# Two of four column blocks of an output projection as seven products of halves, with sums of weights made by DMA during the recurrence

## The chip, the cores and the metric

The kernel runs on one core of one Trainium2 chip. The metric is the device time of one execution in microseconds. The profile is of one execution, taken by the hardware profiler.

## What is computed

One layer of a hybrid trunk over 512 positions of width 2048, in fp32:

```python
h = rms_norm(x, norm_g)
z = h @ w_in                       # r, k, v, two small inputs | gate | pool input | pool gate
y = wkv7_scan(r, decay, k, v, kk, a)              # 16 heads of 64: a recurrence over positions
y_rwkv = (head_group_norm(y) + bonus) * silu(g_rwkv)
y_pool = (causal_multiscale_pool(u) @ w_pool) * pool_scale * silu(g_pool)
x = x + concat([y_rwkv, y_pool]) @ w_out          # 512 x 2048 by 2048 x 2048
x = x + sigmoid(x @ w_pg + b_pg) * (p @ w_ple)
return rms_norm(x, final_g)
```

## The kernel before

**Matmuls.** Every large product is in fp32 by three matmuls (`mm3`, all recorded at line 157): each operand is split into a high part (a cast, on ScalarE) and a low part (the rest, by a subtraction on VectorE), and high x high, high x low and low x high are summed in PSUM. A weight chunk is 256 KB: the sync queue (SP) loads it into `raw` (line 129), ScalarE makes `whi` (line 132), VectorE makes `wlo` (line 133). `raw`, `whi` and `wlo` are rings of four buffers, so a load waits for the `wlo` of the chunk whose slot it takes.

**The recurrence** goes over eight pairs of heads (j = 0 to 7), each in eight chunks of 64 positions. TensorE's instructions are in a fixed order there: short matmuls of the recurrence (`py`, `pu`, `ps`) stand between the matmuls of the input projection for the next pair (`zk`, `zr`, `zv`, `zg`) and for the pooling (`zb`), which `pump` deals out. VectorE's `sbd` (line 809, the state) and `zs` (line 787) are on the way from one chunk to the next, and GpSimd scales the state beforehand (`s0p`, line 816).

During the recurrence of pair j-1, `scores(j)` makes pair j's triangular matrices `mt`. The sync queue writes parts of them to DRAM (`nd`, four DMAs, line 639) and reads them back spread over the partitions (`n`, two DMAs, line 644). `invert(j)` then takes 31 steps on VectorE (`tm` and `xw`, lines 657 and 661), which a scheduler has placed between VectorE's other work. Each engine and each queue works in its own order: what stands behind a waiting instruction waits too.

**The output projection** (`acc_o`) is four column blocks of 512. Each goes over 16 chunks of w_out; a chunk feeds four row tiles by three matmuls, 192 a block. Block 0 also splits the last of the input y (`load_y`: `yin` in six buffers, then `yhi`, `ylo`). After a block VectorE adds x to the four accumulators (line 995), the sums are stored (`x2d`), and `turn` transposes them on TensorE and splits them again (`x2hi`, `x2lo`), for the gate projection `acc_g`. The DMAs of x and `x2d` are issued by ScalarE's queue. GpSimd issues no DMA.

Of the kernel before, what the change touches and what calls it, by code (L numbers as in the profile page):

```python
# [28 lines left out]
O_U, O_GP = O_G + DR, O_G + 2 * DR  # L29
KAPPA = math.exp(-0.5)  # L30
CK = 4


@with_exitstack
def trunk_kernel(ctx: ExitStack, tc: tile.TileContext, x, p, norm_g, w_in, mu, w0, w_up, a0, a_up,
                 k_k, k_a, r_k, ln_w, ln_b, w_pool, pool_scale, w_out, w_ple, w_pg, b_pg, final_g, out):
    nc = tc.nc
# [82 lines left out]
    def dp(o, i):  # L120
        return dprm[:, o + i:o + i + 1]

    hhi = hp.tile([P, KT, T], F32R, name="hhi", tag="ahi")
    hlo = hp.tile([P, KT, T], F32R, name="hlo", tag="alo")


    def wsplit(src, kt, n, nm):
# [39 lines left out]
        return mm(ps, wl, xh, start=False, stop=last)  # L167


    plan, ready = [], {}  # L170

    def plan_cols(c0, nm):
        for c in range(KT // CK):
# [19 lines left out]
    n_ = 0  # L193
# [211 lines left out]
    def pool_unit(n):  # L405
# [31 lines left out]
        nc.vector.scalar_tensor_tensor(sgp, pq, dp(73, m), sgp, ALU.mult, ALU.mult)  # L437
        nc.scalar.dma_start(out=yd[NJ + m], in_=sgp)

    phl, pn = [], []  # L440


# [313 lines left out]
    def recur(j, work, between):  # L756
# [17 lines left out]
        for ch in range(NCH):  # L774
# [42 lines left out]
            if ch % 4 == 3:  # L817
# [13 lines left out]
            step()  # L831
            if ch == 0:
                between()
            else:
                pump(HC3)
# [76 lines left out]
    yhi = ymp.tile([P, KT, T], F32R, name="yhi")  # L912
    ylo = ymp.tile([P, KT, T], F32R, name="ylo")
    AHEAD = 6

    def load_y(k):
        t_ = ymp.tile([P, T], F32, name=f"yin{k}", tag="yin", bufs=AHEAD)
        nc.scalar.dma_start(out=t_, in_=yd[k])
        split(yhi[:, k, :], ylo[:, k, :], t_)

    for k in order[:AHEAD]:
        load_y(k)
# [1 line left out]
    pin[0] = False  # L924


    x2hi = hp.tile([P, KT, T], F32R, name="x2hi", tag="ahi")
    x2lo = hp.tile([P, KT, T], F32R, name="x2lo", tag="alo")
    x2d = dram.tile([T, D], F32, name="x2d", bufs=1)

    KEEP, LATE = 8, 4
# [8 lines left out]
    def proj(w, hi_, lo_, ec, nm, ks=range(KT), tts=range(NT), keep=None, aside=None):  # L940
        acc = {tt: acc_tile(f"acc_{nm}{ec}_{tt}") for tt in tts}
        for i, k in enumerate(ks):
            src = w[k * P:(k + 1) * P, ec * EC:(ec + 1) * EC].unsqueeze(1)
            if nm == "o" and ec == 0 and i + AHEAD < KT:
                load_y(ks[i + AHEAD])
            if (f"{nm}{ec}_{k}", 0) in ready:
                wh, wl = ready.pop((f"{nm}{ec}_{k}", 0))
            elif nm == "o" and ec == 0 and i < 4:
                wh, wl = chunk(f"{nm}{ec}_{k}", 0)
            elif keep is None or LATE <= i < KT - KEEP:  # L950
                wh, wl = wsplit(src, 1, EC, f"{nm}{ec}_{k}")
            else:
                raw = wp.tile([P, 1, EC], F32, name=f"raw_{nm}{ec}_{k}", tag="raw")
                nc.sync.dma_start(out=raw, in_=src)
                if i < 2:
                    if i == 0:
                        two = [pp.tile([P, 2, EC], F32R, name=f"{g}k", tag=g, bufs=1) for g in ("dh", "dl")]
                    wh, wl = (g[:, i:i + 1, :] for g in two)
                else:
                    own = i < KT - 4  # L960
                    wh, wl = ((kp_ if own else wp).tile([P, 1, EC], F32R, name=f"{g}k{k}",
                                                        tag=f"{g}k{k}" if own else g) for g in ("whi", "wlo"))
                split(wh, wl, raw)
                keep[k] = (wh, wl)
                if i >= LATE:
                    continue
            for tt in tts if keep is None or i >= LATE else tts[:-1]:
# [3 lines left out]
            if aside is not None and i == 2:  # L971
                with tc.issue_after(e_.ins):
                    hi = aside()
                with tc.issue_after(hi.ins):
                    recall(0, lp)
        return acc

    ples = {}
# [5 lines left out]
            nc.scalar.dma_start(out=t_, in_=pled[tt * P:(tt + 1) * P, ec * EC:(ec + 1) * EC])  # L984
            ples[ec].append(t_)

    for ec in range(D // EC):
        es = slice(ec * EC, (ec + 1) * EC)
        acc = proj(w_out, yhi, ylo, ec, "o", order)
        x2 = []  # L990
        for tt in range(NT):
            rows = slice(tt * P, (tt + 1) * P)
            t_ = pp.tile([P, EC], F32, name=f"x2_{ec}_{tt}", tag=("u", "sw")[tt // 2])
            nc.scalar.dma_start(out=t_, in_=x[rows, es])
            nc.vector.tensor_tensor(t_, acc[tt], t_, ALU.add)
            nc.scalar.dma_start(out=x2d[rows, es], in_=t_)
            x2.append(t_)
        def turn(ec=ec, x2=x2):
            for i in range(EC // P):
                pt = psM.tile([P, T], F32, name=f"px2_{ec}_{i}", tag="m")  # L1000
                for tt in range(NT):
                    nc.tensor.transpose(pt[:, tt * P:(tt + 1) * P], x2[tt][:, i * P:(i + 1) * P], ident)
                hi = split(x2hi[:, 4 * ec + i, :], x2lo[:, 4 * ec + i, :], pt)
            return hi


        if ec < D // EC - 1:
            turn()

    sy.close()  # L1010

# [1 line left out]
    with tc.tile_pool(name="fp", bufs=2) as fp, tc.tile_pool(name="kp_", bufs=1) as kp_:  # L1013
# [92 lines left out]
        for ec in range(LAST):  # L1106
            pre = {}
            vec = vectors(ec)
            acc = proj(w_pg, x2hi, x2lo, ec, "g", aside=turn if ec == 0 else None)
# [71 lines left out]
```

## Time and profile before

| | |
|---|---|
| median of 3 runs | 1097.62 us (1097.45 to 1099.14) |
| profiled execution | 1097.72 us, its span 1095.9 us |
| granted TensorE clock | 0.998 |
| busy: TensorE, VectorE, ScalarE, GpSimd | 1070.8, 708.2, 448.3, 76.9 us |
| DMA, mean over the span | 126 GB/s |
| output projection | from 728.97 to 909.07 us |

Times in the trace count from the start of the span. A row of a timeline has its start, its length (both in us), the engine, the line, the operation and the tiles (out<-in). In the chain of waits each row starts where the one ahead of it has released it. "SPq" is the time in which the sync queue issues a DMA; "DMA" is the time from issue to landing. A row of the waits has the time in all, the number of times and the longest.

### The profile page before, as it was taken

What the parts mean: (1) busy time and instruction counts of PE and PEld (TensorE: products, weight loads), DVE (VectorE), ACT (ScalarE), POOL (GpSimd) and SP (SyncE); (2) the same over time, 40 slices, a digit from 0 to 9 for tenths busy, and PEclk for the clock granted to TensorE, in tenths of its full rate; (3) what the DMA queues carried; (4) which work ended last, traced back from release to release, by engine and by line L of the source; (5) the groups of instructions that cost most, each with busy time, mean ns of one, the idle gap of its engine ahead of it and who ended that gap; (6) DMA issues with size and microseconds to landing.
All of it is one profiled execution on the core that took longest, in us unless ns stands there. A gap on an engine that the chain in (4) does not pass through costs nothing.

```text
span 1095.9 us, 17196 instructions
## 1 busy us (share of the span) xinstructions
PE 1070.8 (98%) x6060; PEld 877.6 (80%) x6060; DVE 708.2 (65%) x1835; ACT 448.3 (41%) x917; POOL 76.9 (7%) x180
## 2 busy tenths in 40 slices
PE   5999999999999999999999999999999999999996
PEld 4888878887788888788878788888888888888885
DVE  6687867878688679678886956454433424445366
ACT  7633535345335335353343344543222222233337
POOL 2100110110110110100101101000000000000000
PEclk9999999999999999999999999999999999999999
DMA  7433433332423333333334242775534438455534
GB/s 233 116 96 97 111 92 84 96 100 73 120 82 105 104 92 89 96 82 93 91 94 119 79 138 93 232 233 169 172 124 136 167 99 244 137 189 137 181 106 154
DMA packets 178486, 138.56 MB, mean 126 GB/s; under 512 B 34678, under 2 KB 139743, under 8 KB 178399
## 3 DMA queue, kind: packets, MB, share of 16 engines
q1 hardware_dynamic: 157694, 103.89, 32.1%
q10 hardware_dynamic: 20704, 33.56, 9.8%
q8 instruction: 48, 0.79, 0.3%
q14 instruction: 40, 0.32, 0.1%
HBM read 118.02 MB, written 18.87 MB: 125 GB/s over the span
## 4 chain that ended last, share of the span: by engine, by line
PE 86%; DVE 5%; DMA 4%; ACT 3%; issue 1%; SPq 0%; ACTq 0%; DVEq 0%
PE acc_o L157 16%; PE zb L157 14%; PE acc_g L157 14%; PE zv L157 8%; PE zk L157 7%; PE zg L157 7%; PE zr L157 7%; PE py L157 2%; PE pple L157 2%; PE pm L157 1%; PE pu L157 1%; DMA n<-nd 1%; PE pp L157 1%; DMA raw_g<-in_w_pg_dram 1%; PE ps L157 1%
## 5 line engine op out<-in xcount | busy, mean ns | idle before, releaser
L133 DVE TENSOR_TENSOR wlo_g<-raw_g,whi_g 128x512 fp32r<-128x512 f32 x84 | 57.0, 685 | 79.6 <-ACT whi_g L132 76.5
L157 PE MATMUL zb<-hhi,whi_b 128*128 128x512 f32 x256 | 107.0, 418 | 0.0
L133 DVE TENSOR_TENSOR wlo_o<-raw_o,whi_o 128x512 fp32r<-128x512 f32 x64 | 43.9, 690 | 91.4 <-ACT whi_o L132 91.4
L157 PE MATMUL zb<-hhi,wlo_b 128*128 128x512 f32 x256 | 100.5, 393 | 0.0
L157 PE MATMUL acc_o<-whi_o,ylo 128*128 128x512 f32 x256 | 100.2, 391 | 0.0
L157 PE MATMUL acc_o<-whi_o,yhi 128*128 128x512 f32 x256 | 99.9, 390 | 0.0
L157 PE MATMUL zb<-hlo,whi_b 128*128 128x512 f32 x256 | 99.9, 390 | 0.0
L157 PE MATMUL acc_o<-wlo_o,yhi 128*128 128x512 f32 x256 | 99.8, 390 | 0.0
L132 ACT CAST whi_g<-raw_g 128x512 fp32r<-128x512 f32 x84 | 51.9, 620 | 102.7 <-PE acc_g L157 55.4
L157 PE MATMUL acc_g<-whi_g,x2hi 128*128 128x512 f32 x208 | 81.3, 391 | 0.0
L157 PE MATMUL acc_g<-wlo_g,x2hi 128*128 128x512 f32 x208 | 80.9, 389 | 0.0
L157 PE MATMUL acc_g<-whi_g,x2lo 128*128 128x512 f32 x208 | 80.7, 389 | 0.0
L132 ACT CAST whi_o<-raw_o 128x512 fp32r<-128x512 f32 x64 | 39.9, 623 | 97.0 <-PE acc_o L157 96.7
L816 POOL TENSOR_SCALAR s0p<-sbd,pw 64x64 f32<-64x64 f32 x96 | 56.6, 589 | 322.8 <-DVE sbd L809 255.0
L132 ACT CAST whi_b<-raw_b 128x512 fp32r<-128x512 f32 x64 | 39.7, 621 | 86.5 <-PE zv L157 35.4
L133 DVE TENSOR_TENSOR wlo_b<-raw_b,whi_b 128x512 fp32r<-128x512 f32 x64 | 43.8, 685 | 34.2 <-ACT whi_b L132 32.9
L157 PEld LDWEIGHTS zb<-hhi,wlo_b 128*128 128x128 f32 x256 | 48.0, 188 | 11.1
L661 DVE TENSOR_TENSOR xw<-xw,tm 128x60 f32<-128x60 f32 (+24 forms) x248 | 52.1, 210 | 6.8
L157 PEld LDWEIGHTS acc_o<-wlo_o,yhi 128*128 128x128 f32 x256 | 48.1, 188 | 10.3 <-DVE wlo_o L133 0.4
L157 PEld LDWEIGHTS acc_o<-whi_o,yhi 128*128 128x128 f32 x256 | 48.1, 188 | 9.7
L157 PEld LDWEIGHTS acc_o<-whi_o,ylo 128*128 128x128 f32 x256 | 48.1, 188 | 9.8
L157 PEld LDWEIGHTS zb<-hhi,whi_b 128*128 128x128 f32 x256 | 48.2, 188 | 8.5
(285 smaller groups left out, 2550.0 us busy)
## 6 DMA issues: line engine op xcount, KB each, us to landing
raw_b<-in_w_in_dram SPq DMA_DIRECT2D x64, 256.0 KB
raw_o<-in_w_out_dram SPq DMA_DIRECT2D x64, 256.0 KB
raw_g<-in_w_pg_dram SPq DMA_DIRECT2D x64, 256.0 KB
raw_k<-in_w_in_dram SPq DMA_DIRECT2D x32, 256.0 KB
raw_r<-in_w_in_dram SPq DMA_DIRECT2D x32, 256.0 KB
raw_v<-in_w_in_dram SPq DMA_DIRECT2D x32, 256.0 KB
raw_g<-in_w_in_dram SPq DMA_DIRECT2D x32, 256.0 KB
n<-nd SPq DMA_DIRECT2D x16, 256.0 KB
```

What stands on the lines that cost most here:

```text
L132: nc.scalar.copy(hi, raw)
L133: nc.vector.tensor_tensor(lo, raw, hi.bitcast(F32), ALU.subtract)
L157: i = nc.tensor.matmul(*a, **k)
L661: nc.vector.tensor_tensor(xw[:, 0:n_, s + 1:32], xw[:, 0:n_, s + 1:32], tm[:, 0:n_, 0:w_], ALU.add)
L816: nc.gpsimd.tensor_scalar(s0p[hc, :], nxt[hc, hc], pcn[hc], None, ALU.mult)
```

## The change

For blocks 1 and 2, the product of y (as halves of rows, and even and odd chunks) and w_out (even and odd chunks by two blocks) is made of seven products of halves in place of eight. `seven` runs them in four runs: P1 with P2, P5 with P7, P6 with P3, then P4. Each product is 8 chunks by two row tiles by three matmuls. P1, P2 and P3 take plain chunks of w_out; P5, P7, P6 and P4 take sums of chunks, `osum` 1, 3, 2 and 4 in DRAM.

The sums of weights are made during the recurrence. 16 extra chunks of w_out ("neg") go through the ring `raw`; GpSimd multiplies each by -1 in place; the sync queue stores it into three sums or one; then 20 accumulating DMAs on GpSimd's queue add the other chunks. The scheduler places these among the rest of each queue's work. The sums of y (`sab_sums`, `sab_split`) are made on VectorE and ScalarE in block 0. `turn` of blocks 0, 1 and 2 moves into block 3 (at chunks 0, 2 and 5). The DMAs of x and `x2d` of blocks 1 and 2 are issued by GpSimd.

```diff
+    def negate(to, q, src):
+        raw = wp.tile([P, 1, T], F32, name=f"raw_n{to[0]}_{q}", tag="raw")
+        nc.sync.dma_start(out=raw, in_=src)
+        def sign():
+            nc.gpsimd.tensor_scalar(raw, raw, -1.0, None, ALU.mult)
+            owed.append(put)
+        def put():
+            for m in to:
+                nc.sync.dma_start(out=osum[m][q].unsqueeze(1), in_=raw)
+        owed.append(sign)
...
     def chunk(nm, c, ahead=2):
...
             n_, c_, src, kt, w_ = plan.pop(0)
+            for i in range(len(owed)):
+                owed.pop(0)()
+            if n_ == "neg":
+                negate(*c_, src)
+                n_, c_, src, kt, w_ = plan.pop(0)
...
+    negs = [("neg", (to, q), w_out[(2 * q + odd) * P:(2 * q + odd + 1) * P, c * EC:(c + 1) * EC].unsqueeze(1), 1, EC)
+            for q in range(KT // 2) for to, odd, c in (((1, 2, 3), 0, 2), ((4,), 1, 1))]
...
             plan_cols({"r": O_R, "k": O_K, "v": O_V, "g": O_G}[nm] + j * P, f"{nm}{j}")
+            if j > 0 and negs:
+                plan.insert(len(plan) - 1, negs.pop(0))
...
+        for m, src in ((1, (0, c1)), (3, (1, c2)), (2, (1, c2)), (2, (0, c1)), (4, None)):
+            for q in range(0, KT // 2, 2):
+                nc.gpsimd.dma_start(out=at(m, q), in_=at(2, q) if src is None else pairs(w, *src, q),
+                                    accum_op=ALU.add)
...
+        nc.vector.tensor_tensor(r1, a1[:, RH], a2[:, RH], ALU.add)
+        nc.vector.tensor_tensor(r3, a1[:, LH], a1[:, RH], ALU.subtract)
+        nc.vector.tensor_tensor(r2, r1, a1[:, LH], ALU.subtract)
+        nc.vector.tensor_tensor(r4, a2[:, LH], r2, ALU.subtract)
...
+        p1, p2 = run([(rows(0, c1), own(0, 0)), (rows(1, c1), own(1, 0))], [bm, bm, bm, ba],
+                     lambda q: sab_split(2, q))
...
+        p5, p7 = run([(lambda q: osum[1][q], summed(1)), (lambda q: osum[3][q], summed(3))], [bb, bb, bb, ba],
+                     lambda q: sab_split(4, q))
...
+        p6, p3 = run([(lambda q: osum[2][q], summed(2)), (rows(1, c2), summed(4))], [bm, bm, bm, ba])
...
+        p4, = run([(lambda q: osum[4][q], own(1, 1))], [bb, bb])
...
-    for ec in range(D // EC):
...
+    x20 = block_o(0)
+    x21, x22 = seven(1, 2)
+    x23 = block_o(3, {0: lambda: turn(0, x20), 2: lambda: turn(1, x21), 5: lambda: turn(2, x22)})
```

On the sync queue, around the `n` of pair 1 (`raw_g1`, `raw_k2`, `raw_r2` are weight chunks of the input projection, `n321` is `n`), the order before is

```order
L129 DMA raw_g1_3_1200<-in_w_in_dram 128x4x128
L129 DMA raw_k2_0_1206<-in_w_in_dram 128x4x128
L129 DMA raw_k2_1_1224<-in_w_in_dram 128x4x128
L129 DMA raw_k2_2_1230<-in_w_in_dram 128x4x128
L129 DMA raw_k2_3_1248<-in_w_in_dram 128x4x128
L639 DMA nd1_1757<-mt1_1727 32x8x32 x4
L129 DMA raw_r2_0_1254<-in_w_in_dram 128x4x128
L644 DMA n321_0_1762<-nd1_1757 128x1x512
```

and after the change, with a load to be negated (`raw_n1_2`) and its three stores,

```order
L144 DMA raw_k2_0_1235<-in_w_in_dram 128x4x128
L144 DMA raw_k2_1_1254<-in_w_in_dram 128x4x128
L144 DMA raw_k2_2_1260<-in_w_in_dram 128x4x128
L192 DMA raw_n1_2_1278<-in_w_out_dram 128x512
L699 DMA nd1_1816<-mt1_1786 32x8x32 x2
L200 DMA osum1_134<-raw_n1_2_1278 128x512
L200 DMA osum2_135<-raw_n1_2_1278 128x512
L200 DMA osum3_136<-raw_n1_2_1278 128x512
L699 DMA nd1_1816<-mt1_1786 32x8x32 x2
L144 DMA raw_k2_3_1280<-in_w_in_dram 128x4x128
L144 DMA raw_r2_0_1287<-in_w_in_dram 128x4x128
L704 DMA n321_0_1821<-nd1_1816 128x1x512
```

The load and the three stores have moved in ahead of `n`. `raw_n1_2` takes the ring slot of `raw_g1_3`, and `raw_r2_0` takes the slot of `raw_n1_2`: it waits until the three stores have landed. In the same way `raw_r1_1`, `raw_r3_0` and `raw_r4_1` wait ahead of three, one and four of the `nd` stores of pairs 0, 2 and 3.

On GpSimd in the recurrence of pair 2, where before the `s0p` of the chunks stand one behind the other, there is now

```order
L876 TENSOR_SCALAR s0p2_3_3998<-sbd0_576,pw2_2472 64x64 x2
L195 TENSOR_SCALAR raw_n1_7_2269<-raw_n1_7_2269 128x512
L495 DMA osum1_134<-in_w_out_dram 128x2x512
L495 DMA osum2_135<-in_w_out_dram 128x2x512
L876 TENSOR_SCALAR s0p2_4_4086<-sbd1_577,pw2_2472 64x64 x2
L495 DMA osum3_136<-in_w_out_dram 128x2x512
L495 DMA osum2_135<-in_w_out_dram 128x2x512
L876 TENSOR_SCALAR s0p2_5_4159<-sbd0_576,pw2_2472 64x64 x2
```

A multiplication and four accumulating DMAs have come in between; an accumulate waits for the stores of its sum, and the second one on `osum2` for the first.

On VectorE between the second and the third run of `seven` (`wlo_f817` is the last chunk of the second run; `seven5`, `seven7` are accumulators of P5; `x2_...` are loads of x), there is now

```order
L148 TENSOR_TENSOR wlo_f817_9080<-raw_f817_9077,whi_f817_9079 128x512
L148 TENSOR_TENSOR wlo_f1204_9128<-raw_f1204_9125,whi_f1204_9127 128x512
L148 TENSOR_TENSOR wlo_f1214_9140<-raw_f1214_9137,whi_f1214_9139 128x512
L1178 TENSOR_TENSOR a0_9091<-s10_8861,seven5_8877 128x512
L1178 TENSOR_TENSOR a1_9097<-s11_8869,seven7_8878 128x512
L148 TENSOR_TENSOR wlo_f1205_9152<-raw_f1205_9149,whi_f1205_9151 128x512
L1181 TENSOR_TENSOR s10_8861<-s10_8861,s70_9093 128x512
L1181 TENSOR_TENSOR s11_8869<-s11_8869,s71_9099 128x512
L1182 TENSOR_TENSOR s70_9093<-s70_9093,a0_9091 128x512
L1182 TENSOR_TENSOR s71_9099<-s71_9099,a1_9097 128x512
L1188 TENSOR_TENSOR a0_9091<-a0_9091,x2_2_0_9103 128x512
L148 TENSOR_TENSOR wlo_f1215_9164<-raw_f1215_9161,whi_f1215_9163 128x512
```

Two `wlo` of the third run stand ahead of the first subtraction, which waits for P5 to be done; seven operations on the sums stand between the second and the fourth.

More of the change, by code (lines that the diff above doesn't have):

```diff
@@ L31, with __init__, __getitem__ @@
 CK = 4
+class Quarters:
+    def __init__(self, make):
+        self.make, self.tiles = make, {}
+    def __getitem__(self, key):
+        p_, k, c = key
+        if k // 4 not in self.tiles:
+            self.tiles[k // 4] = self.make(k // 4)
+        return self.tiles[k // 4][p_, k % 4, c]
 @with_exitstack
@@ L167, in mm3 @@
         return mm(ps, wl, xh, start=False, stop=last)
-    plan, ready = [], {}
+    plan, ready, owed = [], {}, []
+    osum = {m: dram.tile([KT // 2, P, T], F32, name=f"osum{m}", bufs=1) for m in (1, 2, 3, 4)}
+    def negate(to, q, src):
[8 more added lines that the diff above has]
+        owed.append(sign)
     def plan_cols(c0, nm):
@@ L831, in recur @@
             step()
+            if j >= 4:
+                next(adds, None)
             if ch == 0:
@@ L966, in proj @@
                     continue
+            if nm == "o" and ec == 0 and i % 2 == 1:
+                sab_sums(k // 2)
             for tt in tts if keep is None or i >= LATE else tts[:-1]:
@@ L985, in recall, with residual, keep_x2 @@
             ples[ec].append(t_)
-    for ec in range(D // EC):
-        es = slice(ec * EC, (ec + 1) * EC)
-        acc = proj(w_out, yhi, ylo, ec, "o", order)
+    def residual(ec, tt, pool, by=nc.scalar, **kw):
+        t_ = pool.tile([P, EC], F32, name=f"x2_{ec}_{tt}", **kw)
+        by.dma_start(out=t_, in_=x[tt * P:(tt + 1) * P, ec * EC:(ec + 1) * EC])
+        return t_
+    def keep_x2(ec, tt, t_, by=nc.scalar):
+        by.dma_start(out=x2d[tt * P:(tt + 1) * P, ec * EC:(ec + 1) * EC], in_=t_)
@@ L990, in trunk_kernel, with turn, block_o @@
+    def turn(ec, x2):
+        for i in range(EC // P):
+            pt = psM.tile([P, T], F32, name=f"px2_{ec}_{i}", tag="m")
+            for tt in range(NT):
+                nc.tensor.transpose(pt[:, tt * P:(tt + 1) * P], x2[tt][:, i * P:(i + 1) * P], ident)
+            hi = split(x2hi[:, 4 * ec + i, :], x2lo[:, 4 * ec + i, :], pt)
+        return hi
+    def block_o(ec, aside=None):
+        acc = proj(w_out, yhi, ylo, ec, "o", order, aside=aside)
         x2 = []
         for tt in range(NT):
-            rows = slice(tt * P, (tt + 1) * P)
@@ L993, in trunk_kernel @@
-            t_ = pp.tile([P, EC], F32, name=f"x2_{ec}_{tt}", tag=("u", "sw")[tt // 2])
-            nc.scalar.dma_start(out=t_, in_=x[rows, es])
+            t_ = residual(ec, tt, pp, tag=("u", "sw")[tt // 2])
             nc.vector.tensor_tensor(t_, acc[tt], t_, ALU.add)
-            nc.scalar.dma_start(out=x2d[rows, es], in_=t_)
+            keep_x2(ec, tt, t_)
             x2.append(t_)
[L998 to L1004, printed above, removed]
```

130 lines of the change are left out of this document (119 added, 11 removed).

## The prediction

> **What bounds the kernel now.** I read the busy times first, then the chain of work that ended last, then the waits, and last the timelines of the sync queue, VectorE and TensorE where the chain leaves TensorE.
>
> ```profile
> span 1095.9 us, 17196 instructions
> PE 1070.8 (98%) x6060; PEld 877.6 (80%) x6060; DVE 708.2 (65%) x1835; ACT 448.3 (41%) x917; POOL 76.9 (7%) x180
> ```
>
> TensorE is busy 98% of the span, so matmuls taken out are worth their time only while nothing new keeps TensorE waiting. The chain prints the output projection in four pieces, one for each column block, and the first piece of the gate projection.
>
> ```profile
> 728.97 43.77 PE acc_o L157 x192
> ...
> 777.12 41.06 PE acc_o L157 x181
> ...
> 822.56 41.07 PE acc_o L157 x181
> ...
> 868.01 41.06 PE acc_o L157 x181
> 909.07 8.16 PE acc_g L157 x36
> ```
>
> A block is 192 matmuls in 43.77 us, 0.228 us each, back to back. The list of waits shows how far ahead the weights are there: 47 casts stood waiting for TensorE to free a buffer.
>
> ```profile
> ACT whi_o L132 <- PE acc_o L157: 96.7, 47, 2.1
> ```
>
> In the recurrence the chain leaves TensorE at two places for long: pair 1 and pair 3 of the recurrence, where the sync queue issues the loads `n` late.
>
> ```profile
> 140.09 0.61 DVE wlo_k L133
> ...
> 140.72 0.39 SPq L129
> ...
> 141.29 6.58 DMA n<-nd
> ...
> 147.90 0.20 DVE tm L657
> ...
> 152.72 0.20 DVE zs L787
> ...
> 152.97 0.49 PE pu L157 x2
> ```
>
> ```profile
> 290.11 0.39 SPq L129
> ...
> 290.68 7.09 DMA n<-nd
> ...
> 300.98 0.30 DVE sbd L809
> ...
> 301.33 0.49 PE py L157 x2
> ```
>
> A weight load (line 129) waits on the sync queue for its ring slot, which VectorE's `wlo` frees; `n` is queued behind it; VectorE stands at `tm`, with the recurrence's own `zs` and `sbd` queued behind; TensorE stands at `pu` or `py`. On these chains nothing is spare: each microsecond by which `n` is issued later is one more of TensorE standing still. This queue is what the change lengthens.
>
> **Term 1, matmuls removed.** 7 products of 48 matmuls instead of 2 blocks of 192: 48 fewer, 48 x 0.228 = **-10.9 us**. It is the most that the change can win, 1.0%.
>
> **Term 2, the sync queue in the recurrence.** Sixteen negated blocks go through the ring of four weight buffers. Each takes a load, a GpSimd multiplication and one or three stores (`osum`), all in the sync queue's order, and the slot is free only when the stores have landed. In the new order, at pairs 0 to 3, a load of three stores stands ahead of `n`; a weight load between them waits for the stores to land. For pair 1 it is `raw_r2_0`, directly ahead of `n`; for pairs 0, 2 and 3 it stands ahead of three, one and four of the `nd` stores that `n` reads. The load of the block to be negated takes the slot of the last `wlo_g` ahead of it:
>
> ```profile
> 71.62 0.69 DVE L133 TENSOR_TENSOR wlo_g<-raw_g,whi_g 128x512 fp32r<-128x512 f32 x1
> ...
> 133.90 0.69 DVE L133 TENSOR_TENSOR wlo_g<-raw_g,whi_g 128x512 fp32r<-128x512 f32 x1 [2.05 <-ACT whi_g L132]
> ...
> 206.22 0.68 DVE L133 TENSOR_TENSOR wlo_g<-raw_g,whi_g 128x512 fp32r<-128x512 f32 x1
> ...
> 278.78 0.68 DVE L133 TENSOR_TENSOR wlo_g<-raw_g,whi_g 128x512 fp32r<-128x512 f32 x1
> ```
>
> so it is issued at 72.31, 134.59, 206.90 and 279.46. From issue to landing, 256 KB loads on this queue took
>
> ```profile
> 594.60 5.98 DMA raw_b<-in_w_in_dram
> ...
> 1024.94 4.00 DMA raw_g<-in_w_pg_dram
> 1030.34 3.35 DMA raw_g<-in_w_pg_dram
> ```
>
> I take 4.00 for load and store, the middle row, with 3.35 and 5.98 as ends. The Trainium skill (DMA: Bandwidth & Descriptors, "Anatomy of one DMA — SWDGE (gpsimd) path") puts a transfer at some 2 us and its bytes over 436 GB/s; my estimate from that is 2.6 us for 256 KB, below all three rows, and with it the latenesses below shrink by 2.8 each and the whole sum is -5.3 (1092.4). The multiplication on GpSimd has no row; the nearest are
>
> ```profile
> L660 POOL COPY xw<-i x8: 396/801/2440, 37.5 to 576.0; 128x256 f32<-128x256 f32 x8
> ```
>
> ```profile
> L668 POOL MEMSET x<- 128x512 f32 x8 | 4.2, 526 | 17.2 <-PE pu L157 12.4 <-DMA raw_g<-in_w_in_dram 4.8
> ```
>
> a write of the same size in 0.53 and a copy of half the size in 0.40 to 2.44. I take 1.3 (between 0.53 and twice the copy's median of 0.80) and 0.53 to 2.44 as ends. The same copy taking 0.40 or 2.44 shows that GpSimd is sometimes held up. The Trainium skill (SBUF — State Buffer, "Who interferes with whom") says that a VectorE instruction with two SBUF inputs and a GpSimd instruction that reads SBUF exclude each other; that speaks against this change, and the copy's spread agrees, but no row here shows which of the two waits.
>
> Three stores at 0.39 each put the last issue 0.78 after the first. An `nd` store and the gap to `n` come from pair 0:
>
> ```profile
> 79.48 1.95 SPq L639 DMA_DIRECT2D nd<-mt  x4
> ...
> 82.79 1.22 SPq L644 DMA_DIRECT2D n<-nd  x2
> ...
> 215.52 1.16 SPq L644 DMA_DIRECT2D n<-nd  x2
> ```
>
> 0.49 us an issue, and landed at most 82.79 - 81.43 = 1.36 after the last.
>
> Stores landed = load issued + 4.00 + 1.3 + 0.78 + 4.00 = load issued + 10.08. Then:
> - Pair 1: 144.7. `raw_r2_0` follows then instead of at 140.72: +4.0, all of it on the chain. **+4.0.**
> - Pair 2: 217.0; one weight load (0.39), one `nd` (0.49), its landing (1.36): `n` at 219.2 instead of 215.52, +3.7. VectorE's next state and TensorE's use of it lie 0.76 apart there (below). **+3.0.**
> - Pair 3: 289.5; one load, four `nd` (1.95), 1.36: `n` at 293.2 instead of 290.68. **+2.6.**
> - Pair 0: 82.4; one load, three `nd`, 1.36: `n` at 85.6 instead of 82.79, +2.8. The inverse ends at 118.45 and TensorE uses it at 122.26, 3.8 later: covered, **0**.
>
> ```profile
> 224.63 0.59 DVE L809 SCALAR_TENSOR_TENSOR sbd<-ps,pw,s0p 64x64 f32<-64x64 f32 x2
> ```
>
> ```profile
> 225.98 0.38 PE L157 MATMUL py<-sbd,ar 128*128 128x128 f32 x2
> ```
>
> ```profile
> 118.01 0.44 DVE L734 STREAM_TRANSPOSE y<-x 32x256 f32<-32x256 f32 x1
> ```
>
> ```profile
> 122.26 0.69 PE L157 MATMUL pq<-y,mt 32*32 32x32 f32 x32
> ```
>
> Together **+9.6**. With the short ends (3.35, 0.53, 3.35: 2.07 less at each pair) it is 1.9 + 0.9 + 0.5 = 3.3; with a store of 5.98 and a multiplication of 2.44 (3.1 more) it is 7.1 + 6.1 + 5.7 + 2.1 = 21. A gain is excluded: the order only puts things ahead of `n`. From pair 4 on no negated block is left, and the order is the old one.
>
> **Term 3, the seven products.** A weight chunk of 256 KB now feeds 6 matmuls, 1.37 us, instead of 12. Rows for the small operations:
>
> ```profile
> L133 DVE TENSOR_TENSOR wlo_o<-raw_o,whi_o 128x512 fp32r<-128x512 f32 x64 | 43.9, 690 | 91.4 <-ACT whi_o L132 91.4
> ...
> L995 DVE TENSOR_TENSOR x<-acc_o,x 128x512 f32<-128x512 f32 x16 | 9.9, 682 | 0.0
> ...
> L133 DVE TENSOR_TENSOR wlo_wp<-raw_wp,whi_wp 128x256 fp32r<-128x256 f32 x8 | 3.3, 410 | 1.4 <-ACT whi_wp L132 1.4
> ```
>
> - Between the second and third run, VectorE has two `wlo` ready ahead, then two subtractions that wait for P5, then ten additions with a few `wlo` strewn in. Counted at 0.6 us a piece back to back, the fourth `wlo` ends 4.5 us after the run's end (needed at 4.1) and the fifth at 6.9 (needed at 6.0): **+1.5**; nothing to 4, since six additions also wait for loads issued by GpSimd.
> - Between the third run and P4, eight additions stand ahead of the fourth `wlo`: ready at 5.8, needed at 4.1: **+1.7** (0.5 to 2.5).
> - Block 0 carries the sums of y: 64 pieces of 0.41 beside 26 `wlo`/`ylo` of 0.69 and 4 additions, 47 us of records, some 41 back to back, in 43.8. I take **+1.0** (0 to 4).
> - The moved transposes are as many as before and lie beside weights that are ahead: 0. The ring's cycle is 5.40 us with a landing of 4.00 (the two `raw_g` rows above, 1024.94 and 1030.34, are one slot's loads), for four chunks, and TensorE needs four in 5.47: 0, with no room left (a rival).
>
> Together **+4.2**.
>
> **Sum.** -10.9 + 9.6 + 4.2 = +2.9. The profiled execution took 1097.72 (span 1095.9 and 1.8 around it); the median of the runs shown is 1097.62. 1097.7 + 2.9 = **1100.6 us**. A measurement of this kernel can tell about 0.2%, 2.2 us, from no change.
>
> **Rivals.**
> - *The stores are quick (faster).* Stores land in the shortest row's time and GpSimd multiplies as fast as it fills: 3.3 from term 2, and the combinations of term 3 cost 2. -10.9 + 5.3 = -5.6: **1092**. The point from which it decides: give-backs below 8.7 us. For it: 3.35 is a measured row, and stores are not loads; against it: three stores are 768 KB at once, where all rows show one load.
> - *GpSimd's queue delays the state (slower).* The accumulating DMAs stand between the `s0p` of GpSimd. In the recurrence of pair 2, after the `n` of pair 3, the last negated block of three stores waits for `wlo_r` at 306.69; plus 5.3, 0.78 and 4.00 the stores have landed at 316.8; an accumulate that must land ahead of the next (at `n`'s 6.58) ends at 323.4, `s0p` 1.4 later, and VectorE uses it at 325.85. It fits by 1 us; with accumulates of twice that time it misses by 5.6, and the multiplications too come late by what blocks them: **1106**.
>
> ```profile
> 306.02 0.67 DVE L133 TENSOR_TENSOR wlo_r<-raw_r,whi_r 128x512 fp32r<-128x512 f32 x1
> ...
> 325.85 0.28 DVE L809 SCALAR_TENSOR_TENSOR sbd<-ps,pw,s0p 64x64 f32<-64x64 f32 x1 [0.70 <-PE ps L157]
> ```
>
> - *The ring of four is too short (slower).* If a load in the seven products lands after 5.0 us instead of 4.0, the cycle is 6.4, 1.61 a chunk: 56 x 0.24 = 13.4, less the four chunks that lie ready (5.5): +7.9, **1108**. For it: a 5.98 row; against it: loads landed in 3.35 to 4.00 where the ring was the limit.
>
> **Numbers.** Forecast 0.43 (its own range 1096 to 1105: same 0.14, slower 0.25, faster 0.04); quick stores 0.32 (faster 0.27, same 0.05); GpSimd's queue 0.15 (slower 0.13, same 0.02); short ring 0.10 (slower 0.09, same 0.01). Faster 0.31, same 0.22, slower 0.47. The range goes from 1091.5, just past the quick case, to 1109, past both slow ones.
>
> **What would show it.** The row to look at first:
>
> ```profile
> DVE tm L657 <- DMA n<-nd: 17.3, 8, 3.8
> ```
>
> Right: 48 fewer matmuls; VectorE's waits at `tm` for `n` grow by about 10 us, at pairs 1 to 3; the chain leaves TensorE there for longer; the seven products take 336 x 0.228 = 76.6 us and some 3 us of gaps at two places. Wrong: stores that land in under 3 us; `n` issued at the old times; gaps in TensorE before `py` with VectorE waiting for GpSimd; or casts waiting for weight loads all through the seven products.

## The result, and the profile after

The changed kernel takes 1137.78 us (median of 4 runs, 1134.03 to 1138.17), the kernel before 1097.86 us beside it: a ratio of 1.0354, interval [1.033, 1.0377]. It is 39 us slower where +2.9 was forecast, and lies outside the range. The profiled execution took 1134.03 us, its span 1132.3.

The page of the changed kernel: the busy times, the queue of GpSimd's DMAs (packets, MB, share of the DMA engines) and the traffic:

```profile
span 1132.3 us, 17567 instructions
...
PE 1075.5 (95%) x6012; PEld 874.7 (77%) x6012; DVE 758.2 (67%) x1941; ACT 475.6 (42%) x977; POOL 133.0 (12%) x232
...
q0 software_dynamic: 6720, 14.68, 6.6%
...
HBM read 138.99 MB, written 37.75 MB: 156 GB/s over the span
```

48 matmuls are gone (6060 to 6012), yet TensorE is busy for longer, 1075.5 us in place of 1070.8. So there are two losses: TensorE stands still more, and what it does takes longer.

To see where, the recurrence and the projection are taken apart. First the stretch from the first pair's `pm` to the first matmul of the output projection, by windows, of before and of after (the length, then the busy time of PE, PEld, DVE, ACT and POOL, then the granted clock, the DMA engines' share and GB/s):

```profile
75.47:728.80 653.33, 649.83 (x4107) 529.72 (x4107) 494.67 (x1457) 274.88 (x590) 67.55 (x115) 1.00 0.37 106
```

```profile
75.19:767.57 692.38, 661.22 (x4108) 536.63 (x4107) 497.48 (x1455) 274.11 (x588) 115.98 (x153) 0.98 0.50 134
```

The same 4107 matmuls take 39.0 us more. TensorE stands still for 692.38 - 661.22 = 31.2 us in place of 3.5: +27.7. The other 11.4 are in the matmuls themselves. The output projection, from 767.57 to the first `acc_g`, takes 178.6 us in place of 180.1. The whole loss is in the recurrence, and the projection wins 1.5 in place of the 6.7 that terms 1 and 3 give together.

The waits of after that answer to the row which the prediction said to look at first:

```profile
DVE tm L717 <- DMA n<-nd: 37.1, 8, 9.1
...
PE py L172 <- DVE sbd L869: 20.6, 8, 7.0
ACT whi_f L147 <- DMA raw_f<-in_w_out_dram: 20.1, 10, 4.7
...
DVE sbd L869 <- POOL s0p L876: 1.6, 1, 1.6
```

`tm` waits 19.8 us more for `n`, twice the 10 named. The longest wait is 9.1 in place of 3.8. TensorE stands at `py` behind it, and in the seven products casts wait for loads. VectorE's `sbd` waits for GpSimd's `s0p` only once, for 1.6 us, so the rival in which GpSimd's queue delays the state is not what costs.

The chain of waits of after, in pairs 0 to 3:

```profile
111.11 9.29 DMA raw_b<-in_w_in_dram
...
120.50 0.62 ACT whi_b L147
...
121.67 0.59 ACT bkn L760
...
122.31 1.22 PE pss L172 x2
...
152.54 1.95 POOL raw_n L195
...
155.37 2.66 DMA osum<-raw_n
...
158.61 6.60 DMA n<-nd
...
271.16 10.99 DMA raw_b<-in_w_in_dram
...
352.80 10.35 DMA raw_b<-in_w_in_dram
```

The rows from 152.54 to 158.61 are the prediction's own term 2: the multiplication, the stores, their landing, and only then `n`. The loads of `raw_b` aren't in the prediction. A weight load of 256 KB lands after 9.29 us, and in pairs 2 and 3 after 10.99 and 10.35; the prediction's rows had 3.35 to 5.98. GpSimd's timeline shows what is beside the first of them, with windows after it, of the whole stretch first and then of its end and what follows:

```profile
109.35 3.74 POOL L495 DMA_DIRECT2D osum<-in_w_out_dram  x3 [2.40 <-DMA osum<-raw_n]
120.69 1.13 POOL L495 DMA_DIRECT2D osum<-in_w_out_dram  x1 [7.60 <-DMA osum<-in_w_out_dram]
```

```profile
109.00:122.00 13.00, 6.73 (x62) 5.27 (x60) 8.51 (x19) 5.21 (x11) 4.87 (x4) 0.97 1.02 204
117.00:122.30 5.30, 0.08 (x4) 0.00 (x0) 1.44 (x3) 1.78 (x4) 1.13 (x1) 0.91 1.12 212
122.30:126.00 3.70, 3.69 (x9) 2.93 (x10) 1.50 (x3) 2.27 (x7) 0.00 (x0) 0.50 1.18 270
126.00:130.00 4.00, 4.00 (x15) 3.19 (x14) 0.71 (x2) 0.65 (x2) 0.00 (x0) 0.73 0.74 156
```

Three accumulating DMAs are issued at once, as soon as the stores that they add to have landed. They are not in pairs 4 to 7, from where the code calls for them; the scheduler has put them as early as they could go (the last is issued at 384.67). The 16 DMA engines are then busy throughout (share 1.02), though they move only 204 GB/s. TensorE stands for 5.23 us from 117.08 on. It stands at `pss`, which needs ScalarE's `bkn`, and ScalarE stood before that at the cast of the late chunk (`whi_b`). When TensorE starts again its clock is granted at 0.50, and 9 matmuls take 3.69 us. That is 0.41 each, where the prediction counted 0.228.

### The profile page after: what moved, and what is told of

It is laid out like the page before. It is cut to its first block, busy times and chain, and to the rows that moved or that the text cites. A ratio compares the mean times of both kernels' runs of the same rounds, so it can differ in the third digit from the quotient of the medians.

```text
span 1132.3 us, 17567 instructions
## 1 busy us (share of the span) xinstructions
PE 1075.5 (95%) x6012; PEld 874.7 (77%) x6012; DVE 758.2 (67%) x1941; ACT 475.6 (42%) x977; POOL 133.0 (12%) x232
## 3 DMA queue, kind: packets, MB, share of 16 engines
q1 hardware_dynamic: 168062, 122.77, 36.3%
HBM read 138.99 MB, written 37.75 MB: 156 GB/s over the span
## 4 chain that ended last, share of the span: by engine, by line
PE 66%; issue 11%; DMA 10%; DVE 8%; ACT 3%; SPq 1%; POOL 1%; ACTq 0%; DVEq 0%; POOLq 0%
PE acc_g L172 14%; PE zb L172 11%; PE zk L172 7%; PE zv L172 6%; PE zg L172 6%; PE zr L172 5%; PE acc_o L172 4%; DMA raw_b<-in_w_in_dram 3%; DMA n<-nd 2%; PE py L172 2%; PE pple L172 1%; PE pu L172 1%; PE pm L172 1%; DMA osum<-raw_n 1%; DMA x<-in_x_dram 1%
## 5 line engine op out<-in xcount | busy, mean ns | idle before, releaser
L148 DVE TENSOR_TENSOR wlo_f<-raw_f,whi_f 128x512 fp32r<-128x512 f32 x56 | 37.4, 691 | 29.1 <-ACT whi_f L147 28.9
L147 ACT CAST whi_f<-raw_f 128x512 fp32r<-128x512 f32 x56 | 34.5, 621 | 52.5 <-DMA raw_f<-in_w_out_dram 20.1
L717 DVE TENSOR_TENSOR tm<-xw,n 128x60 f32<-128x60 f32 (+10 forms) x240 | 51.9, 216 | 6.4
L172 PE MATMUL zk<-hhi,whi_k 128*128 128x512 f32 x128 | 55.2, 431 | 0.0
L172 PEld LDWEIGHTS zb<-hlo,whi_b 128*128 128x128 f32 x256 | 48.8, 190 | 8.0
L172 PE MATMUL zv<-hhi,whi_v 128*128 128x512 f32 x128 | 54.4, 425 | 0.0
L172 PE MATMUL zr<-hhi,whi_r 128*128 128x512 f32 x128 | 53.5, 418 | 0.0
L172 PE MATMUL zg<-hhi,whi_g 128*128 128x512 f32 x128 | 52.6, 411 | 0.0
```

Source lines behind the costliest of these rows:

```text
L147: nc.scalar.copy(hi, raw)
L148: nc.vector.tensor_tensor(lo, raw, hi.bitcast(F32), ALU.subtract)
L172: i = nc.tensor.matmul(*a, **k)
L717: nc.vector.tensor_tensor(tm[:, 0:n_, 0:w_], xin[:, 0:n_, s:s + 1].to_broadcast([P, n_, w_]), nb[s // 16][:, s % 16:s % 16 + 1, s + 1:32]. ...
```

## The experiments

**What each part costs.** Three kernels leave parts out, so that the loss falls into pieces.

*No accumulates.* Everything else stays.

```diff
-    adds = added(osum, w_out, 1, 2)
+    adds = iter(())
```

> The 20 accumulating DMAs are left out (the sums of weights then lack their added chunks); loads, multiplications, stores and the seven products stay. Theory A (while accumulating DMAs are in flight, the weight loads beside them land after 9 to 11 us instead of 3 to 4, and GpSimd's other work stands behind them): the 13 us lost ahead of pair 1 go, and half of the 9 to 10 us each at pairs 2 and 3: about 1115 us. Theory B (on record: the stores stand ahead of n in the sync queue, the accumulates cost next to nothing): within 3 us of the changed kernel, 1134 to 1138 us.

Measured: 1111.23 us (1110.67 to 1115.98), ratio 1.0128 [1.0093, 1.0163]. The accumulates cost 1.0354 - 1.0128 = 2.3%, some 25 us, two thirds of the loss. That fits theory A, which gave about 1115 us, and not theory B. The recurrence of this kernel is where term 2 stands alone. Its row of the windows, from `pm` to the projection:

```profile
75.07:744.51 669.44, 656.32 (x4107) 534.04 (x4107) 496.52 (x1455) 273.75 (x588) 92.00 (x133) 0.99 0.43 123
```

The stretch takes 669.44 - 653.33 = 16.1 us more than before. TensorE stands for 13.1 us in place of 3.5, which is +9.6, as much as term 2 gave. The matmuls take 6.5 more. The wait at `tm`, and the chain of pair 1:

```profile
DVE tm L717 <- DMA n<-nd: 27.5, 8, 5.4
```

```profile
136.65 3.06 DMA raw_n<-in_w_out_dram
...
139.88 1.51 POOL raw_n L195
...
142.27 2.65 DMA osum<-raw_n
...
145.00 0.40 SPq L144
...
145.50 6.60 DMA n<-nd
```

The wait has grown by 10.2 us. From the load's issue to the store's landing it takes 145.00 - 136.65 = 8.35 us (10.08 forecast).

The accumulates had also made this path longer. In pairs 2 and 3 of the changed kernel the load to be negated is multiplied 7.0 and 7.3 us after its issue, with an accumulate issued 1.7 and 3.1 us ahead of it; here it is 3.5 us both times. TensorE then stands at `py` for 6.8 and 7.0 us there, and for 2.8 and 3.2 us here.

*The seven products alone.* No negated blocks and no accumulates; all chunks are plain ones of w_out.

```diff
-            if j > 0 and negs:
+            if False:
...
-    adds = added(osum, w_out, 1, 2)
+    adds = iter(())
...
-        p5, p7 = run([(lambda q: osum[1][q], summed(1)), (lambda q: osum[3][q], summed(3))], [bb, bb, bb, ba],
+        p5, p7 = run([(rows(0, c1), summed(1)), (rows(1, c2), summed(3))], [bb, bb, bb, ba],
```

(and so for P6 and P4)

> Nothing is added to the recurrence: no loads to be negated, no stores, no accumulates; the seven products read plain chunks of w_out in place of the sums. Both theories: what the change does from the output projection on stays, 180.1 us before and 178.4 us after, so 1096 us. If it is 1087 to 1090 us, the sums read from DRAM were what slows the seven products; if it is above 1100 us, the output projection shares in the loss.

Measured: 1100.68 us (1099.22 to 1104.16), ratio 1.0027 [1.0011, 1.0042]. With nothing at all in the recurrence the products are 0.27% slower, not 0.6% faster. The wait of the casts, the seven products by windows, and the chain in their first run:

```profile
ACT whi_f L147 <- DMA raw_f<-in_w_out_dram: 41.7, 23, 6.2
```

```profile
772.87:861.07 88.20, 80.42 (x338) 62.28 (x337) 53.00 (x84) 36.05 (x60) 6.45 (x12) 1.00 0.66 207
```

```profile
777.64 4.84 DMA raw_f<-in_w_out_dram
...
782.58 0.62 ACT whi_f L147
...
783.26 0.63 ACT whi_f L147
...
783.91 0.70 DVE wlo_f L148
...
784.63 3.61 DMA raw_f<-in_w_out_dram
...
790.38 4.22 DMA raw_f<-in_w_out_dram
```

The chain goes round the ring: load, cast, `wlo`, load. Rounds take 6.99 and 5.75 us, since two loads land together and the second cast stands behind the first. TensorE uses up four chunks in 5.47. This is the rival of the short ring.

The expectation missed: the projection takes 182.8 us here, and 178.6 in the changed kernel. There, 32 of the 56 loads in the seven products read sums from `osum`, and the seven products are shorter:

```profile
811.58:896.38 84.80, 80.14 (x337) 62.20 (x336) 53.52 (x85) 36.33 (x60) 6.46 (x12) 1.00 0.68 217
```

So this kernel overstates by some 4 us what the products lose in the changed one. Why loads of plain chunks hold them up longer isn't shown.

*Loads and multiplications without stores.* The negated blocks are loaded and multiplied but not stored; nothing is added; the seven products read plain chunks.

```diff
         def sign():
             nc.gpsimd.tensor_scalar(raw, raw, -1.0, None, ALU.mult)
-            owed.append(put)
```

> The 16 loads through the ring and the multiplications on GpSimd stay; the 32 stores and the 20 accumulates are left out, and the seven products read plain chunks of w_out. Theory B: with the stores gone, n is issued nearly as before; what stays is a ring slot held through a load and a multiplication: 1097 to 1102 us. Theory A: the stores are cheap beside the accumulates, so this is as e1, about 1110 to 1115 us.

Measured: 1106.33 us (1103.32 to 1107.88), ratio 1.007 [1.005, 1.0091]. Against the seven products alone, loads and multiplications cost 0.4% and the stores with the reads of `osum` 0.6%. The projection takes 182.3 us here and 178.4 in the kernel without accumulates, which reads `osum`; so the stores alone cost about 0.9% (an estimate from these times). Both count; neither is the whole of term 2, and the time lies between the two expected.

**Why the accumulates cost so much.**

*Copies in their place.* The same DMAs, at the same places, without the addition.

```diff
-                nc.gpsimd.dma_start(out=at(m, q), in_=at(2, q) if src is None else pairs(w, *src, q),
-                                    accum_op=ALU.add)
+                nc.gpsimd.dma_start(out=at(m, q), in_=at(2, q) if src is None else pairs(w, *src, q))
```

> The changed kernel with its 20 accumulating DMAs made plain copies of the same blocks at the same places in the same queue (the sums are then not sums). A copy moves each byte twice (read, written), an accumulate three times. If the bytes in the DMA queues are what costs: 1111 plus two thirds of 26.5 us, 1126 to 1130 us. If it is the accumulation itself (reading and writing the same place): at most 1117 us. If it is that GpSimd stands at their waits and issues: 1134 to 1138 us, as the changed kernel.

Measured: 1120.16 us (1118.63 to 1125.7), ratio 1.0221 [1.019, 1.025]. A copy still costs: 0.9% over no DMA at all. The addition costs another 1.3%. The time lies between the three expected, so none of these causes is the whole cost. The page's issues of copies, of accumulates in the changed kernel, and the copies' window beside the first group:

```profile
osum<-in_w_out_dram POOLq DMA_DIRECT2D x16, 512.0 KB, 6.2
```

```profile
osum<-in_w_out_dram POOLq DMA_DIRECT2D x16, 512.0 KB, 8.4
```

```profile
112.00:122.00 10.00, 5.11 (x51) 4.03 (x50) 7.37 (x13) 6.50 (x15) 0.69 (x1) 0.97 1.02 310
```

and the same window with accumulates:

```profile
112.00:122.00 10.00, 3.82 (x45) 3.01 (x45) 5.69 (x11) 4.94 (x10) 2.22 (x2) 0.97 1.09 202
```

With copies the busy DMA engines move 310 GB/s, with accumulates 202. The page counts the same traffic for both, 138.99 MB read and 37.75 written, so the price of the addition isn't in the bytes that it counts. Whether the read of the destination is missing from that count, these runs don't show.

*One at a time, later.* The accumulates stand behind the scaling of the state (`s0p`), one a chunk, in pairs 4 to 7.

```diff
+                        g_ = nc.gpsimd.tensor_scalar(s0p[hc, :], nxt[hc, hc], pcn[hc], None, ALU.mult)
+                    if j >= 4:
+                        with tc.issue_after(g_.ins):
+                            next(adds, None)
...
-            if j >= 4:
-                next(adds, None)
```

> The whole computation; the accumulates are kept behind the states that GpSimd scales in pairs 4 to 7, one to each, where the queue holds no more loads to be negated. Theory A: pair 1 no longer loses 13 us and pairs 2 and 3 lose half, and one accumulate at a time crowds little: 1112 to 1120 us; if each accumulate delays the weight loads beside it wherever it stands, 1125 us or more. Theory B: 1134 us as before.

Measured: 1118.38 us (1117.55 to 1118.81), ratio 1.0183 [1.0154, 1.0211]: the accumulates cost 0.6% in place of 2.3%, with the same bytes. So what costs is when they are issued, not that they are. This kernel spreads them and also moves them away from the negated blocks; it doesn't tell the two apart.

**What the ring costs.**

*Eight buffers.* Of the seven products alone, every second chunk is loaded into four other buffers.

```diff
+                    turns[0] += 1
+                    more = (lp, dict(tag="ple", bufs=4)) if turns[0] % 2 else (None, {})
```

> As e2 (seven products of plain chunks, nothing added to the recurrence), with every second chunk of the seven products loaded into four more buffers, a ring of eight in place of four. Theory R (the ring of four is what stops TensorE in the seven products: 11.5 us of pauses in e2, most of them at casts that wait for a load): some 3 to 4 us of pauses stay, at VectorE's additions, and the time is 1092 to 1094 us. If VectorE's additions between the runs are the limit: 1099 to 1101 us, as e2.

Measured: 1097.86 us (1094.95 to 1102.57), ratio 1.0009 [0.9994, 1.0023], between the two expected. The seven products shrank to 79.6 us as expected, but block 0 grew from 44.5 to 50.6, and the whole did not win. Four of the new loads were free to go and went ahead of block 0's own (at 720.99 to 725.44). The chain of block 0 then shows loads of y, which took 4.34 and 4.11 us one behind the other:

```profile
746.10 4.34 DMA yin<-yd
750.52 4.11 DMA yin<-yd
```

*Eight buffers, loads in order.* Each load of the seven products stands behind the one ahead of it on the sync queue ("the run before it" is the run with eight buffers).

```diff
-                    wh, wl = wsplit(src(q).unsqueeze(1), 1, EC, f"f{len(made)}{i}{q}", more[0], **more[1])
+                    with tc.issue_after(loads[-1].ins):
+                        wh, wl = wsplit(src(q).unsqueeze(1), 1, EC, f"f{len(made)}{i}{q}", more[0], **more[1])
```

> The seven products on plain chunks with a ring of eight, as in the run before it, but each of their loads stands behind the one ahead of it on the sync queue, so that none is issued in block 0. Theory (seven products win 6 to 8 us once the ring does not stop them, and block 0 grew to 50.6 us because four of their loads crowded its own): block 0 falls back to 44 to 45 us, the seven products stay at 79 to 80, the whole comes to 1091 to 1093 us, ratio about 0.995. Rival (the pauses are owed by the products and only move from one block to another): block 0 falls back, the seven products go back to 84 us or more, and the whole stays at 1096 to 1099 us.

Measured: 1092.2 us (1092.08 to 1093.5), ratio 0.9948 [0.9936, 0.9961]. Block 0 takes 45.9 us and the seven products:

```profile
774.58:855.16 80.58, 77.61 (x338) 62.62 (x336) 54.11 (x85) 36.75 (x60) 6.45 (x12) 1.00 0.69 219
```

TensorE stands for 3.0 us there in place of 7.8, mainly in two pauses (1.73 and 0.94), at the additions between the runs. This is faster than the kernel before, by 5.7 us without the sums of weights; so that is all that the sums may cost.

**The whole change, arranged otherwise.** Five kernels make the sums of weights in other places.

*Eight buffers with the late accumulates*, loads not in order: the edits of the two kernels together.

> The whole computation, e4 (accumulates late) with the ring of eight of e5. Theory R: 4 to 5 us of the 8.5 us of pauses go, 1113 to 1115 us. If the seven products are limited otherwise: 1118 us as e4.

Measured: 1117.62 us (1113.85 to 1118.28), ratio 1.0191 [1.0174, 1.0208]: no gain over the ring of four, as with the products alone. Block 0 grew to 50.9 us.

*Negated blocks kept behind `n`.* They go only among the chunks of v and of the pooling, so into all pairs, and the accumulates of four blocks follow as soon as these are stored, behind the scaling of the state in any pair. The seven products have eight buffers. The main lines of the edit:

```diff
-            if j > 0 and negs:
+            if j > 0 and nm == "v" and negs:
...
                 plan_cols(O_U + g * 256 + i * P, f"b{j}")
+                if negs:
+                    plan.insert(len(plan) - 1, negs.pop(0))
```

> The whole computation, with the ring of eight; the blocks to be negated are loaded among the weights of v and of the pooling only, so that no store stands ahead of an n, and the accumulates of two blocks are issued as soon as both are stored, spread over pairs 1 to 7. Queue theory (my term 2): the 10.6 us that loads, multiplications and stores cost in e3 and e1 fall to 2 or 3; the accumulates cost 5 to 8 as in e4; the seven products win 7: 1097 to 1102 us. If the accumulates cost by crowding wherever three are issued together, not by what stands at n: 1108 us or more.

Measured: 1134.13 us (1128.74 to 1136.33), ratio 1.0332 [1.0302, 1.0362], not the 1097 to 1102 us of the queue theory. The accumulates of a group were issued together again. GpSimd's timeline, and from the chain a store of 32 KB beside them:

```profile
576.91 1.20 POOL L502 DMA_DIRECT2D osum<-in_w_out_dram  x1 [2.15 <-DMA osum<-raw_n]
579.68 2.48 POOL L502 DMA_DIRECT2D osum<-in_w_out_dram  x2 [1.56 <-DMA xd<-xw]
588.62 1.14 POOL L502 DMA_DIRECT2D osum<-in_w_out_dram  x1 [6.46 <-DMA osum<-in_w_out_dram]
```

```profile
581.90 11.03 DMA xd<-xw
```

What `invert` has made goes through this store on its way to TensorE, which stands for 3.35 us from 592.85. Two more long gaps have other causes. From 596.48 it stands for 4.82 us, where VectorE does a reciprocal ahead of its second `y`. From 482.98 it stands for 4.36: VectorE's `sbd` waits for GpSimd's `s0p`, which stands behind an accumulate that waits for another. Such waits come to 7.6 us in this kernel, so the rival of GpSimd's queue does act here. All this hid what the kernel was made to show; the next three take it apart.

*Late accumulates, eight buffers, loads in order.* The edits of three kernels above together.

> The whole change with the accumulating DMAs one at a time behind the scaling of the state, the ring of eight and the loads in order. Theory (the parts add up): front 10.6 + accumulates 7 + back -6 on 1097.5 = 1109 to 1112 us, ratio 1.011 to 1.013, so still slower than before. Rival (the loss of the front and of the accumulates is hidden or made up elsewhere once the back runs freely): under 1105 us.

Measured: 1110.6 us (1108.34 to 1113.0), ratio 1.0106 [1.009, 1.0121]. The parts add up.

*No negated block ahead of `n`.* Blocks go among the chunks of r, v and g, not k. The accumulates go by row blocks, once the four negated blocks of each are stored. All else is as in the kernel before this one.

```diff
-            if j > 0 and negs:
+            if j > 0 and nm != "k" and negs:
...
-        for m, src in ((1, (0, c1)), (3, (1, c2)), (2, (1, c2)), (2, (0, c1)), (4, None)):
-            for q in range(0, KT // 2, 2):
+        for q in range(0, KT // 2, 2):
+            for m, src in ((1, (0, c1)), (3, (1, c2)), (2, (1, c2)), (2, (0, c1)), (4, None)):
+                while len(stored) < 2 * q + 4:
+                    yield
```

> As the run before it (whole change, accumulating DMAs one at a time, ring of eight, loads in order), but no negated block among the chunks of k, which stand ahead of the n loads on the sync queue; they go to r, v and g, three a pair, and the accumulates of a row block follow once its four blocks are stored. In the run before it the matmuls of the fifth pair started 16.9 us late. Theory (what the front costs is n issued late behind stores that a weight load waits for): that lateness falls below 7 us, and the whole comes to 1098 to 1102 us, ratio 0.999 to 1.004. Rival (it is the ring itself: sixteen more chunks in four slots, and their traffic, wherever they stand): the fifth pair still starts 13 us late or more, and the whole stays at 1108 to 1112 us.

Measured: 1105.7 us (1104.01 to 1107.55), ratio 1.0079 [1.0066, 1.0091]. The fifth pair's `pm`, in TensorE's timeline of the run before it and of this one (359.69 in the kernel before), and the wait at `tm` in this one:

```profile
376.21 2.06 PE L172 MATMUL pm<-ar,bk 64*128 64x128 f32 x32
```

```profile
361.20 2.06 PE L172 MATMUL pm<-ar,bk 64*128 64x128 f32 x32
```

```profile
DVE tm L720 <- DMA n<-nd: 19.4, 8, 5.0
```

The lateness fell from 16.5 us to 1.5, though by then only 12 of the 16 blocks have gone through the ring, at three a pair. The whole is still 4 us above the top of what was expected: pairs 4 to 7 lose 11 us. Half of that isn't the accumulates' doing. Pair 4 takes 80.1 us in place of 74.3, and the first accumulate is issued at its end, at 438.64: TensorE stands for 3.67 us from 424.45 because one of VectorE's two `y` stands behind a reciprocal of 3.35 us, where in the kernel before both stand ahead of it. In pair 5 the store of the last block (issued at 447.49) stands ahead of three of the `nd` after all, and TensorE stands for 2.88 us at `py`: term 2 again.

*All blocks stored before pair 4.* Blocks among r, v, b and g, four a pair; late accumulates by sums, as in the run with the loads in order (the "tied loads"). Eight buffers and loads in order stay.

```diff
-            if j > 0 and negs:
+            if j > 0 and nm != "k" and negs:
...
                 plan_cols(O_U + g * 256 + i * P, f"b{j}")
+                if negs:
+                    plan.insert(len(plan) - 1, negs.pop(0))
```

> As the run before it, with the negated blocks among the chunks of r, v, b and g, four a pair, so that all are stored before pair 4, and the accumulates by sums, one behind each scaling of the state in pairs 4 to 7, as in the run with the tied loads. Theory (front nearly free when nothing stands ahead of n; accumulates, no longer beside the negated blocks, cost the 4.4 us that pairs 4 to 7 lost with the tied loads; the back wins 5): the fifth pair starts 1 to 4 us late, pairs 4 to 7 lose 4 to 5 us more, the whole comes to 1097 to 1100 us, ratio 0.999 to 1.003. Rival (the accumulates cost 11 us, as in the run before it, whatever stands beside them): 1104 us or more.

Measured: 1099.19 us (1096.4 to 1102.69, 12 runs), ratio 1.0017 [1.0005, 1.003]. The profiled execution took 1096.84 us, near the lower end. Its windows, from the first `pm` and from the fifth pair's `pm` to the projection; then the second stretch of the kernel before:

```profile
75.10:734.22 659.12, 651.01 (x4107) 529.68 (x4107) 499.09 (x1456) 274.51 (x590) 119.18 (x153) 1.00 0.53 141
362.41:734.22 371.81, 368.17 (x2287) 299.77 (x2287) 272.15 (x815) 155.81 (x336) 61.60 (x89) 1.00 0.58 143
```

```profile
359.69:728.80 369.11, 367.88 (x2287) 299.74 (x2287) 272.60 (x816) 155.98 (x336) 36.42 (x67) 1.00 0.39 114
```

The fifth pair starts 2.7 us late, with all 16 blocks stored, and `tm` waits 17.9 us for `n` in place of 17.3. So the loss of the front is `n` issued late, not the blocks in the ring. The 20 accumulates in pairs 4 to 7 cost 371.81 - 369.11 = 2.7 us (4.4 at the same places in the kernel with the tied loads). The 16 negated blocks in pairs 0 to 3 cost about as much (659.12 - 653.33 - 2.7 = 3.1), and the projection, 175.0 us in place of 180.1, gives 5.1 back. The same work that lost 39 us loses about 2 when it is placed otherwise and the ring has eight buffers. None of the kernels with the whole change beat the kernel before.

## Why the prediction was wrong, step by step

The direction was right. The size was wrong by a cost that the sum leaves out.

**The accumulates: the step that failed.** The sum has no term for the 20 accumulating DMAs. They come up only in the rival "GpSimd's queue delays the state", with a size of 1106, by their place between the `s0p`. The runs show another cause and over four times the size: they are issued in groups as soon as they are ready, fill the DMA engines, and weight loads beside them land after 9.29 to 10.99 us. Without them the kernel is 2.3% faster; one at a time they cost 0.6% in the first kernel made so and 2.7 us in the last. The order ahead of the prediction already has four of them close together in pair 2. Their price stands in no row of the kernel before, where GpSimd issues no DMA.

**Term 2, the sync queue: right in mechanism, its total in part by luck.** The forecast was +9.6. Without accumulates TensorE stands for 9.6 us more and `tm` waits 10.2 us more. But the pairs 0 to 3 were forecast at 0, 4.0, 3.0 and 2.6 of that, and TensorE's standing grew by 1.8, 1.7, 2.8 and 2.7 us, with 0.7 behind them. Shorter loads and stores (3.06, 1.51 and 2.65 in pair 1) were made up for by pair 0, forecast at nothing. In time the front cost 16.1 us, not 9.6, for the reason that follows. That `n` is the path was shown by keeping the blocks from ahead of it: the fifth pair then starts 2.7 us late, and 15.0 late in the kernel without accumulates.

**The clock: left out.** Most of the long gaps also slow the matmuls behind them. The same 4107 matmuls took 6.5 us more without accumulates and 11.4 more in the changed kernel, with a granted clock of 0.50 behind the gap of 5.23. The prediction priced a wait at its own length.

**Term 3, the ring: "0, with no room left" was wrong.** A forecast of -6.7 for terms 1 and 3 came out at -1.5 in the changed kernel (the projection by the windows) and at +3 with plain chunks, both with a ring of four. With eight buffers it came out at -5.7 (ratio 0.9948), so **term 1** and the rest of term 3 hold: the pauses at the additions were 1.73 and 0.94 (forecast +1.5 and +1.7). The rival of the short ring had the mechanism; its cycle of 6.4 lies between the 5.75 and 6.99 seen, and its price of 7.9 us was above the 4.8 by which the pauses grew. Nothing in the rows then excluded it, and it got a chance of 0.10.

**The sum.** By the windows of the profiled executions: accumulates 692.38 - 669.44 = +22.9, the rest of the front +16.1 (forecast +9.6), the projection -1.5 (forecast -6.7), all else -1.2; together the 36.3 us between 1097.72 and 1134.03. The *quick stores* came true as well: they landed in 2.65 us, under the 3 that was to show the forecast wrong, and that helped little. The estimate of 2.6 us that stands beside the prediction's sum rests on a section about DMAs that GpSimd issues; on the sync queue it fits the stores (2.65), not the loads (3.06 and more).

## What to carry to other kernels

A DMA whose result isn't needed soon still has a price where others need the DMA engines: ask where the order lets it be issued, and spread what is not urgent one at a time. When a chunk feeds half the work, ask again whether the ring is deep enough (here four buffers left pauses of 7.8 us and eight 3.0), and keep its loads in order so that the new ones don't pass the old. Where a queue carries an input of the critical path, what is put ahead of that input counts; what is put behind it cost little here (3.1 us for 16 blocks).

## What was not expected of the hardware

- **Half clock after some short gaps.** In the changed kernel the granted clock was 0.50 behind a gap of 5.23 us, and in the stretch with a gap of 1.82 us (from 136.31) it was lower too:

```profile
138.00:142.00 4.00, 3.87 (x11) 3.15 (x12) 1.96 (x4) 1.10 (x4) 2.62 (x1) 0.57 0.32 95
```

  Behind a gap of 2.04 us (from 750.87) in the kernel with eight buffers and loads in order it was not:

```profile
752.91:756.90 3.99, 3.99 (x18) 3.30 (x18) 3.99 (x10) 3.32 (x9) 0.00 (x0) 1.00 0.81 261
```

  The Trainium skill (TensorE: Matmul & The Clock Gate, "Part 1: The HAM clock gate") says that the clock falls to half after an idle window of some 3.4 us and comes back after as long a busy one. The return agrees: 0.50 for 3.7 us, then 0.73 over the next 4. A gap of 1.82 us that is enough does not. The length alone doesn't decide, as the longer gap of 2.04 shows; what does, these runs don't show.
- **Accumulates from DRAM to DRAM** of 512 KB landed after 8.4 us in crowds (median; copies 6.2), and the DMA engines, busy throughout the ten microseconds shown, moved 202 GB/s with them and 310 with copies.
- **GpSimd's multiplication** of 128 x 512 in place took 1.50 us in the changed kernel (the median of 16), at most 2.63, and once 6.06 in the last kernel (records of GpSimd are rough); 0.53 to 2.44 was the bound.
